# The opening of a four-layer decoder: one list of steps for all engines, two more pieces of weights ahead of the second tokens, two subtractions on GpSimd

## The chip, the cores and the metric

The kernel runs on one core of a Trainium2 chip. What counts is the device time of one execution in microseconds. Five engines run their own instruction streams in order: TensorE (matrix products and transposes), VectorE, ScalarE, GpSimd, and SyncE, which here only issues transfers from HBM. They wait for each other through semaphores.

## The reference

The whole trunk is four layers over 256 tokens of 1024 values. A layer is a token mixer (attention, short convolution, gated linear attention, attention again) and a squared-ReLU MLP, each between two RMS norms:

```python
def reference(x, norm_gains, sb_w_qkv, ...):
    h = x
    for i in range(DEPTH):
        kind, j = i % N_MIXERS, i // N_MIXERS
        xn = rms_norm(h, norm_gains[i, 0])
        ...
        h = h + rms_norm(m, norm_gains[i, 1])
        f = squared_relu_mlp(rms_norm(h, norm_gains[i, 2]), ffn_w_up[i], ffn_w_down[i])
        h = h + rms_norm(f, norm_gains[i, 3])
    return h
```

The change lies in the opening: the first norm (`rms_norm(h, norm_gains[0, 0])`) and the first of layer 0's projections, `xn @ w_qkv` for the values, columns 2048 to 3071 of `sb_w_qkv[0]`.

## The kernel before, in words

Everything is in float32. To run products at the fast rate, each operand is split into two parts of lower precision, a rounded upper part (`hi`) and the rest (`lo = raw - hi`), and a product of two matrices becomes three: hi with hi, hi with lo, lo with hi. Weights stream from HBM in pieces of 128 x 1024 (half a megabyte). Each piece lands in one of five `raw` buffers (`next_piece`, line 204, transfer on SyncE's queue at line 219), ScalarE casts it to `hi` (line 232), VectorE subtracts to `lo` (line 242), both in two halves of 512 columns, and TensorE takes the parts from rings of nine buffers. A raw buffer comes free when the subtractions of its piece are done, and only then its next transfer starts.

The 256 tokens are two groups of 128 (`h[0]` and `h[1]`, "first" and "second" tokens below). In the opening (`opening`, line 1008) each group is loaded; its sum of squares is taken half by ScalarE (`sumsq`, line 294) and half by VectorE (line 1034); one over the root follows (`rstd_on_act`: a small addition on GpSimd, line 287, then Ln and Exp on ScalarE, lines 288 and 289; for the second group `rstd_of`: line 277 on VectorE and a power on GpSimd, line 278); VectorE scales the group (line 1040), TensorE turns it in two halves of four 128 x 128 transposes (line 323) into PSUM, ScalarE rounds it with the gains to `xth` (line 1050) and VectorE forms the rest `xtl` (line 1057). Then the value projection runs: 8 pieces of weights, 2 groups, three kinds of products (hh: `xth` with `hi`; hl: `xth` with `lo`; lh: `xtl` with `hi`), and two halves of 512 columns, 96 products in all, into two accumulators of PSUM. Where nothing real is ready, TensorE runs fillers (`keep_busy`), products of a tile of ones with a tile of zeros. GpSimd fills four tiles with zeros at the start (line 581) and is almost idle after.

The order of the opening on VectorE, ScalarE, TensorE and SyncE is the order in which the code is written, inside `tc.manual_schedule`; the rest of the kernel is ordered by the scheduler. After the opening come the queries' and keys' projections, which start with piece 8 of the weights.

The lines of the opening that set the order around the change:

```python
            pieces.append(next_piece())
            nc.sync.dma_start(out=h[1], in_=xv[1])
            upper(0)
            pieces[0][1](0)
            first, second = halves_squared(1)
            pieces[0][1](1)
            r = rstd_of(first, 1, second)
            rounded(0, 0)
            rest_of(0, 0)
            in_order("hh00 hl00 lh00")
            normed(1, 0, r)
            normed(1, 1, r)
```

## Time and profile before

| what | us |
|---|---|
| median of three runs | 1175.03 (1174.85 to 1176.07) |
| the profiled execution | 1174.96 |
| span of its instructions | 1173.2 |
| TensorE busy | 1164.6 (99%) |
| VectorE busy | 813.5 (69%) |
| ScalarE busy | 678.1 (58%) |
| GpSimd busy | 43.8 (4%) |
| first product of the opening starts | 8.95 |
| first product of the queries starts | 32.04 |

The span is the time from the first to the last instruction of the program. The rows further down are of five kinds: the page's busy shares, the timelines of single engines (consecutive instructions of one line are merged into a row with their count), groups of instructions with their mean length, the range of lengths of one line's instructions, and the time from a transfer's issue to its landing.

### The profile page before, as it was taken

How to read it: one execution, taken by the hardware profiler on the slowest of the kernel's cores; microseconds unless marked ns; L12 is line 12 of the kernel's file. 1: busy time of each engine (PE TensorE's matmuls, PEld its weight loads, DVE VectorE, ACT ScalarE, POOL GpSimd, SP SyncE). 2: the span in 40 equal slices, each digit the busy share in tenths (PEclk: the TensorE clock that was granted, in tenths of full speed). 3: DMA queues.
4: the chain of work that ended last, by engine and by line, in shares of the span. 5: the costliest groups of instructions: out<-in, count | busy, mean ns of one | idle time of the engine just before them, and what ended most of it. 6: DMA issues, size and time to landing. Idle time of an engine off the chain costs nothing.

```text
span 1173.2 us, 17278 instructions
## 1 busy us (share of the span) xinstructions
PE 1164.6 (99%) x6424; PEld 1004.0 (86%) x6424; DVE 813.5 (69%) x1299; ACT 678.1 (58%) x1255; POOL 43.8 (4%) x84
## 2 busy tenths in 40 slices
PE   9999999999999999999999999999999999999997
PEld 7998888888888888888889888888888998888886
DVE  7875876664877786665777778657658776855652
ACT  6886655543655564554584756545546875644541
POOL 1000100000100100000101010000000001000000
PEclk9999999999999999999999999999999999999999
DMA  8743676666576476666473536666647444666640
GB/s 270 240 145 106 187 243 185 195 194 181 168 237 204 146 235 196 185 195 220 143 228 107 178 122 217 194 191 193 208 147 230 135 144 135 222 192 191 190 149 36
DMA packets 126185, 213.65 MB, mean 182 GB/s; under 512 B 10955, under 2 KB 89043, under 8 KB 126101
## 3 DMA queue, kind: packets, MB, share of 16 engines
q1 hardware_dynamic: 125620, 211.95, 58.1%
q8 instruction: 50, 0.82, 0.3%
q10 hardware_dynamic: 448, 0.59, 0.1%
q14 instruction: 35, 0.28, 0.1%
q0 software_dynamic: 32, 0.00, 0.0%
HBM read 211.48 MB, written 1.05 MB: 181 GB/s over the span
## 4 chain that ended last, share of the span: by engine, by line
PE 97%; ACT 1%; DMA 0%; DVE 0%; issue 0%; SPq 0%; DVEq 0%; ACTq 0%
PE acc L119 71%; PE wk L119 24%; PE wk L323 2%; ACT hi L234 0%; DMA h<-in_x_dram 0%; ACT hi L232 0%; ACT s L944 0%; ACT s L294 0%; DVE s L829 0%; DVE lo L242 0%; ACT s L268 0%; ACT s L819 0%; ACT s L817 0%; SPq L219 0%; SPq L130 0%
## 5 line engine op out<-in xcount | busy, mean ns | idle before, releaser
L242 DVE TENSOR_TENSOR lo<-raw,hi 128x512 fp32r<-128x512 f32 x752 | 491.8, 686 | 207.2 <-ACT hi L232 204.4
L232 ACT CAST hi<-raw 128x512 fp32r<-128x512 f32 x752 | 438.4, 620 | 313.2 <-PE acc L119 172.1
L119 PE MATMUL acc<-hi,s 128*128 128x512 f32 x1216 | 339.5, 391 | 0.1
L119 PEld LDWEIGHTS acc<-hi,s 128*128 128x128 f32 x1216 | 225.1, 188 | 46.1 <-ACT s L268 0.8
L119 PE MATMUL wk<-xt,hi 128*128 128x256 f32 (+1 forms) x1120 | 248.7, 309 | 0.0
L119 PE MATMUL wk<-xt,lo 128*128 128x256 f32 x704 | 196.9, 280 | 0.0
L119 PEld LDWEIGHTS wk<-xt,hi 128*128 128x128 f32 x1120 | 181.8, 188 | 13.4 <-ACT s L805 0.3
L119 PE MATMUL acc<-lo,s 128*128 128x512 f32 x608 | 190.4, 390 | 0.0
L119 PE MATMUL acc<-xt,hi 128*128 128x512 f32 x512 | 179.6, 393 | 0.0
L119 PE MATMUL acc<-hi,xt 128*128 128x512 f32 x576 | 159.9, 394 | 0.1
L119 PE MATMUL acc<-xt,lo 128*128 128x256 f32 x512 | 143.2, 280 | 0.0
L119 PEld LDWEIGHTS acc<-lo,s 128*128 128x128 f32 x608 | 114.0, 188 | 23.8
L119 PEld LDWEIGHTS wk<-xt,lo 128*128 128x128 f32 x704 | 132.3, 188 | 0.0
L119 PEld LDWEIGHTS acc<-hi,xt 128*128 128x128 f32 x576 | 106.2, 188 | 23.1 <-ACT xt L268 1.4
L119 PEld LDWEIGHTS acc<-xt,hi 128*128 128x128 f32 x512 | 96.1, 188 | 21.0
L119 PEld LDWEIGHTS acc<-xt,lo 128*128 128x128 f32 x512 | 96.2, 188 | 0.9
L119 PE MATMUL acc<-lo,xt 128*128 128x512 f32 x288 | 89.2, 391 | 0.0
L119 PEld LDWEIGHTS acc<-lo,xt 128*128 128x128 f32 x288 | 54.0, 188 | 11.4
L309 DVE TENSOR_TENSOR s<-acc,s 128x1024 f32<-128x1024 f32 (+1 forms) x16 | 19.0, 1190 | 57.5 <-ACT s L294 57.3
L275 POOL TENSOR_SCALAR sm<-sm 128x1 f32<-128x1 f32 x29 | 13.7, 471 | 1038.5 <-ACT s L294 1038.5
L294 ACT ACTIVATE s<-acc 128x1024 f32<-128x1024 f32 (+1 forms) x16 | 16.0, 999 | 55.4 <-PE acc L119 55.4
L119 PE MATMUL acc<-s,s 128*128 128x256 f32 (+4 forms) x298 | 39.3, 317 | 0.4 <-DVE s L829 0.2
(136 smaller groups left out, 882.2 us busy)
## 6 DMA issues: line engine op xcount, KB each, us to landing
raw<-in_ffn_w_up_dram SPq DMA_DIRECT2D x128, 512.0 KB, 4.0
raw<-in_ffn_w_down_dram SPq DMA_DIRECT2D x128, 512.0 KB, 3.7
raw<-in_sb_w_qkv_dram SPq DMA_DIRECT2D x47, 512.0 KB, 4.8
raw<-in_conv_w_in_dram SPq DMA_DIRECT2D x24, 512.0 KB, 4.8
raw<-in_gla_w_in_dram SPq DMA_DIRECT2D x24, 512.0 KB, 3.9
raw<-in_sb_w_o_dram SPq DMA_DIRECT2D x16, 512.0 KB, 3.9
s<-in_norm_gains_dram SPq DMA_DIRECT2D x15, 512.0 KB, 5.5
raw<-in_conv_w_out_dram SPq DMA_DIRECT2D x8, 512.0 KB, 4.3
```

The lines of the kernel that those rows point to most:

```text
L119: nc.tensor.matmul(out=o, lhsT=l, rhs=r, start=start, stop=stop, skip_group_check=True)
L232: nc.scalar.copy(out=hi[:, cs], in_=raw[:, cs])
L242: nc.vector.tensor_tensor(out=lo[:, cs], in0=raw[:, cs], in1=hi[:, cs].bitcast(F32), op=ALU.subtract)
L275: nc.gpsimd.tensor_scalar(out=v, in0=ss, scalar1=EPS, scalar2=None, op0=ALU.add)
L294: nc.scalar.activation(out=scratch()[:, 0:src.shape[1]], in_=src, func=AF.Square, scale=1.0 / 32.0, accum_out=ss)
L309: nc.vector.tensor_tensor(out=ag[:, cs], in0=a, in1=g[:, cs], op=ALU.mult)
L323: nc.tensor.transpose(out=dst[:, j * P:(j + 1) * P], in_=src[:, j * P:(j + 1) * P], identity=ident)
```

## The change

The opening is now driven by one string, `ORDER`. Each word is a step: `ld` a piece's transfer, `h00` the transfer of the second tokens, `q` half a sum of squares, `r` the root, `n` a scaling, `f` four transposes, `g` and `gt` the gains' transpose and copy, `z` fillers, `u` and `d` one rounding and one rest of 128 columns, `hi` and `lo` one half of a cast and of a subtraction, `po` a subtraction on GpSimd, and `hh`, `hl`, `lh` one product (piece, group of tokens, half). GpSimd is now among the engines whose order is the list's. Two lines of the table stand for it:

```diff
+ORDER = " ".join((
+    "ld00 ld10 ld20 h00 ld30 ld40 q0a q0b z06 g00 r00 n00 gt00 hi00 z02 f00 lo00 hi01 u00 n01 u01 lo01 ld50 hh000 u02",
+    "hh001 u03 hl000 hi10 d00 hl001 f01 d01 hi11 d02 lh100 d03 hi20 lo10 lh101 po11 ld60 hh100 hi21 hh101 lh000 lh001",
...
-    for cs in (slice(0, 512), slice(512, D)):
+
+    cuts = [(slice(0, n), slice(n, D)) for n in (640, 512)]
+    for cs in cuts[0]:
         nc.sync.dma_start(out=h[0][:, cs], in_=xv[0][:, cs])
     cfl = T(cp, [P, C_A], F32, "cf")
-    nc.scalar.dma_start(out=cfl[:, 0:P], in_=const_f[:, 0:P])
+    nc.sync.dma_start(out=cfl[:, 0:P], in_=const_f[:, 0:P])
...
-        def lower(j):
+        def lower(j, eng=nc.vector):
...
-            nc.vector.tensor_tensor(out=lo[:, cs], in0=raw[:, cs], in1=hi[:, cs].bitcast(F32), op=ALU.subtract)
-
-        return upper, lower
+            eng.tensor_tensor(out=lo[:, cs], in0=raw[:, cs], in1=hi[:, cs].bitcast(F32), op=ALU.subtract)
+
+        return upper, lower, partial(lower, eng=nc.gpsimd)
...
+        def product(which, t, k, n):
+
+
+            seen[t, n] = seen.get((t, n), 0) + 1
+            mm(banks(accs[t])[n], xs(t)[which == "lh"][k], wide((l, "v"), k)[n][which == "hl"],
+               seen[t, n] == 1, seen[t, n] == 3 * KT)
+
+        def step(word):
...
+            elif what == "r":
+                factor[t] = rstd_on_act(sums[t, "b"], 1, sums[t, "a"])
...
+            elif what in ("u", "d"):
+                (rounded if what == "u" else rest_of)(t, int(at[1]))
+            elif what in ("hi", "lo", "po"):
+                pieces[t][("hi", "lo", "po").index(what)](int(at[1]))
...
         with tc.manual_schedule(engines={mybir.EngineType.DVE, mybir.EngineType.Activation, mybir.EngineType.PE,
-                                         mybir.EngineType.SP}):
+                                         mybir.EngineType.SP, mybir.EngineType.Pool}):
             nc.vector.memset(still.bitcast(F32), 0.0)
-            keep_busy(STILL[0])
...
+            for word in ORDER.split():
+                step(word)
             rest_of_constants()
             ahead[0] = RAMP[0]
```

So the transfers go out as: first tokens (640 and 384 columns), the identity's constants, pieces 0, 1 and 2, second tokens, pieces 3 and 4; before, they were first tokens (512 and 512), piece 0, second tokens, pieces 1, 2 and on, with the constants on ScalarE's queue. The fillers are 6 + 2 instead of 5 + 4 + 4. The root of the second tokens now takes the way of the first (addition on GpSimd, Ln and Exp on ScalarE). The second halves of pieces 1 and 2 are subtracted on GpSimd. The number of products, transposes, casts and roundings is the same. After the opening, the instructions of each engine stand in the order of before but for a half cast or two.

On GpSimd, from the last of the four fills on, this stands before (`sm` are columns of 128 single values; L287 is the addition for the first tokens, L278 the power for the second, L275 already belongs to the end of the layer's mixer):

```order
L581 MEMSET s_103 128x1024
L287 ISA
L287 TENSOR_SCALAR sm_134<-sm_128 128x1 [waits Activation_49]
L278 TENSOR_TENSOR sm_169<-sm_170,mhalf_91 128x1 [waits DVE_49]
L275 TENSOR_SCALAR sm_1379<-sm_1374 128x1 [waits Activation_49]
```

and this now (L305 is the addition, for the first tokens and for the second; L260 the subtraction; raw_121 and raw_125 are pieces 1 and 2):

```order
L599 MEMSET s_103 128x1024
L305 ISA
L305 TENSOR_SCALAR sm_152<-sm_138 128x1 [waits Activation_49]
L260 TENSOR_TENSOR lo_124<-raw_121,hi_123 128x512 [waits DMAHW6_49,Activation_49]
L260 TENSOR_TENSOR lo_128<-raw_125,hi_127 128x512 [waits DMAHW7_49,Activation_49]
L305 TENSOR_SCALAR sm_223<-sm_208 128x1 [waits Activation_49]
```

The two subtractions stand between the additions of the first and of the second tokens.

On VectorE, from the gains' copy to the second tokens' scaling, this stands before (h_80 and h_81 are the first and second tokens, sm_110 the gains, raw_154 piece 0, wk_139 the first turned half of the first tokens):

```order
L1093 COPY sm_110<-wk_121 128x8 [waits PE_49]
L1034 SCALAR_TENSOR_TENSOR s_106,sm_131<-h_80 128x512 [waits DMAHW1_49]
L1040 TENSOR_SCALAR s_111<-h_80,sm_133 128x512 [waits DMAHW0_49,Activation_49]
L1040 TENSOR_SCALAR s_111<-h_80,sm_133 128x512
L242 TENSOR_TENSOR lo_158<-raw_154,hi_157 128x512 [waits DMAHW3_49,Activation_49]
L1034 SCALAR_TENSOR_TENSOR s_106,sm_166<-h_81 128x512 [waits DMAHW6_49,DVE_49]
L242 TENSOR_TENSOR lo_158<-raw_154,hi_157 128x512 [waits DMAHW5_49,Activation_49]
L277 TENSOR_SCALAR sm_170<-sm_163,sm_166 128x1 [waits DVE_49,Activation_49]
L1057 SCALAR_TENSOR_TENSOR xt_94<-wk_139,sm_110,xt_94 128x128 [waits Activation_49]
L1057 SCALAR_TENSOR_TENSOR xt_94<-wk_139,sm_110,xt_94 128x128 x3
L1040 TENSOR_SCALAR s_112<-h_81,sm_169 128x512 [waits Pool_49]
```

and this now (raw_116, raw_121 and raw_125 are pieces 0, 1 and 2, wk_161 the first turned half):

```order
L1089 SCALAR_TENSOR_TENSOR s_106,sm_141<-h_80 128x384 [waits DMAHW1_49]
L1095 TENSOR_SCALAR s_111<-h_80,sm_151 128x512 [waits DMAHW0_49,Activation_49]
L1106 COPY sm_110<-wk_149 128x8 [waits PE_49]
L260 TENSOR_TENSOR lo_120<-raw_116,hi_119 128x512 [waits DMAHW4_49,Activation_49]
L1095 TENSOR_SCALAR s_111<-h_80,sm_151 128x512
L260 TENSOR_TENSOR lo_120<-raw_116,hi_119 128x512 [waits DMAHW5_49,Activation_49]
L1057 SCALAR_TENSOR_TENSOR xt_94<-wk_161,sm_110,xt_94 128x128 [waits DVE_49,Activation_49]
L1057 SCALAR_TENSOR_TENSOR xt_94<-wk_161,sm_110,xt_94 128x128 x3
L260 TENSOR_TENSOR lo_124<-raw_121,hi_123 128x512 [waits DMAHW6_49,Activation_49]
L1089 SCALAR_TENSOR_TENSOR s_106,sm_211<-h_81 128x512 [waits DMAHW0_49]
L260 TENSOR_TENSOR lo_128<-raw_125,hi_127 128x512 [waits DMAHW7_49,Activation_49]
L1095 TENSOR_SCALAR s_112<-h_81,sm_222 128x512 [waits Activation_49]
```

The gains' copy moved behind the first scaling, and the second tokens' squares (s_106 from h_81) moved behind the rests of the first tokens and the first subtraction of piece 1.

On TensorE, ahead of the second tokens' first transposes, this stands before (acc_107 is the accumulator of the first tokens, hi_157 and hi_191 belong to pieces 0 and 1, wk_199 is the second tokens' first turned half; two products stand in front of these rows):

```order
L119 MATMUL acc_107<-lo_158,xt_94 128x512 [waits DVE_49] x2
L119 MATMUL acc_107<-hi_157,xt_94 128x512 [waits DVE_49]
L119 MATMUL acc_107<-hi_157,xt_94 128x512
L119 MATMUL acc_107<-hi_191,xt_94 128x512 [waits Activation_49] x2
L119 MATMUL acc_107<-hi_191,xt_94 128x512 [waits DVE_49]
L119 MATMUL acc_107<-hi_191,xt_94 128x512
L323 MATMUL wk_199<-cf_84,s_112 128x128 [waits DVE_49]
```

and this now (hi_119, hi_123 and hi_127 belong to pieces 0, 1 and 2, wk_234 is the second tokens' first turned half; four products and the four transposes of the first tokens' second half stand in front of these rows):

```order
L135 MATMUL acc_107<-hi_123,xt_94 128x512 [waits DVE_49,Activation_49]
L135 MATMUL acc_107<-hi_123,xt_94 128x512 [waits Activation_49]
L135 MATMUL acc_107<-hi_123,xt_94 128x512 x2
L135 MATMUL acc_107<-hi_119,xt_94 128x512 x2
L135 MATMUL acc_107<-hi_127,xt_94 128x512 [waits DVE_49,Activation_49]
L135 MATMUL acc_107<-hi_127,xt_94 128x512 [waits Activation_49]
L135 MATMUL acc_107<-lo_124,xt_94 128x512 [waits DVE_49]
L135 MATMUL acc_107<-lo_124,xt_94 128x512 [waits Pool_49]
L135 MATMUL acc_107<-hi_127,xt_94 128x512 x2
L135 MATMUL acc_107<-lo_128,xt_94 128x512 [waits DVE_49]
L135 MATMUL acc_107<-lo_128,xt_94 128x512 [waits Pool_49]
L341 MATMUL wk_234<-cf_84,s_112 128x128 [waits DVE_49]
```

All products of pieces 0, 1 and 2 that need only the first four slices of the first tokens now stand ahead of the second tokens' transposes, 18 instead of 10, and two of them wait for GpSimd.

## Rows read from the trace of the kernel before

**Rows 1.** The page's first part: busy us, share of the span, count.

```profile
PE 1164.6 (99%) x6424; PEld 1004.0 (86%) x6424; DVE 813.5 (69%) x1299; ACT 678.1 (58%) x1255; POOL 43.8 (4%) x84
```

**Rows 2.** Timeline of TensorE, 0 to 45: start, length, instruction, count, [idle].

```profile
1.84 2.50 PE L119 MATMUL acc<-s,onesr 128*128 128x512 f32 x5 [1.84 <-DVE s L1089]
...
4.48 2.08 PE L119 MATMUL acc<-s,onesr 128*128 128x512 f32 x4
6.56 1.41 PE L323 MATMUL wk<-cf,s 128*128 128x128 f32 x8
...
8.95 0.73 PE L119 MATMUL acc<-hi,xt 128*128 128x512 f32 x2
...
28.87 0.62 PE L119 MATMUL acc<-lo,xt 128*128 128x512 f32 x2
29.32 1.07 PE L119 MATMUL acc<-hi,xt 128*128 128x512 f32 x4
...
32.04 0.40 PE L119 MATMUL wk<-xt,hi 128*128 128x256 f32 x2
```

**Rows 3.** Timeline of ScalarE in the opening.

```profile
5.46 0.29 ACT L288 ACTIVATE sm<-sm,sm 128x1 f32<-128x1 f32 x1 [1.07 <-DVE s L1034]
...
6.67 0.62 ACT L232 CAST hi<-raw 128x512 fp32r<-128x512 f32 x1 [0.18 <-DMA raw<-in_sb_w_qkv_dram]
7.92 0.63 ACT L294 ACTIVATE s<-h 128x512 f32<-128x512 f32 x1 [0.63 <-DMA h<-in_x_dram]
...
8.55 1.12 ACT L1050 ACTIVATE xt<-wk,sm 128x128 fp32r<-128x128 f32 x4
9.55 2.19 ACT L232 CAST hi<-raw 128x512 fp32r<-128x512 f32 x4
```

**Rows 4.** Timeline of VectorE in the opening.

```profile
1.02 0.73 DVE L140 CAST onesr<-mones 128x128 fp32r<-128x128 f32 x1
...
4.58 0.17 DVE L1093 COPY sm<-wk 128x8 f32<-128x8 f32 x1 [2.79 <-PE wk L1092]
4.67 0.68 DVE L1034 SCALAR_TENSOR_TENSOR s<-h 128x512 f32<-128x512 f32 x1
...
6.02 0.88 DVE L1040 TENSOR_SCALAR s<-h,sm 128x512 f32<-128x512 f32 x2 [0.66 <-ACT sm L289]
...
25.35 0.22 DVE L1006 CAST cr<-cf 128x128 fp32r<-128x128 f32 x1
```

**Rows 5.** Landing of the first tokens' second half: issue, and time from it.

```profile
L130 SPq DMA_DIRECT2D h<-in_x_dram x1: 420/420/420, 1.2 to 1.2; - x1
...
DMA to landing us min/median/max: 3.2/3.2/3.2
```

**Rows 6.** Landing of piece 2, the same view.

```profile
L219 SPq DMA_DIRECT2D raw<-in_sb_w_qkv_dram x1: 328/328/328, 3.7 to 3.7; - x1
...
DMA to landing us min/median/max: 6.7/6.7/6.7
```

**Rows 7.** GpSimd's groups: busy us, mean ns, idle; the last alone at 614.

```profile
L581 POOL MEMSET s<- 128x1024 f32 x4 | 3.7, 970 | 0.3 <-POOLq L1173 0.3
...
L287 POOL TENSOR_SCALAR sm<-sm 128x1 f32<-128x1 f32 x2 | 0.4, 221 | 4.2 <-ACT s L294 4.1
...
L858 POOL TENSOR_SCALAR s<-s 128x64 f32<-128x64 f32 x1 | 0.5, 458 | 0.3 <-ACT s L854 0.3
```

**Rows 8.** Timeline of GpSimd, 881 to 883.

```profile
881.44 1.15 POOL L275 TENSOR_SCALAR sm<-sm 128x1 f32<-128x1 f32 x1 [3.44 <-ACT s L294]
```

**Rows 9.** Timeline of VectorE in the same stretch.

```profile
880.69 1.21 DVE L332 TENSOR_TENSOR s<-h,s 128x1024 f32<-128x1024 f32 x1
881.83 0.68 DVE L242 TENSOR_TENSOR lo<-raw,hi 128x512 fp32r<-128x512 f32 x1
```

**Rows 10.** Timeline of GpSimd in the opening: the four fills.

```profile
0.72 3.69 POOL L581 MEMSET s<- 128x1024 f32 x4 [0.29 <-POOLq L1173]
```

**Rows 11.** Line 899 on VectorE: shortest, median, longest in ns, first, last start.

```profile
L899 DVE TENSOR_TENSOR s<-s,s x28: 412/418/458, 620.8 to 642.5; 128x256 f32<-128x256 f32 x28
```

More of the change, by code (lines that the diff above doesn't have):

```diff
@@ L1061, in opening @@
-        pieces = []
-        def upper(*js):
-            for j in js:
-                while len(pieces) <= j:
-                    pieces.append(next_piece())
-                for n in range(PS):
-                    pieces[j][0](n)
-        def lower(*js):
-            for j in js:
-                for n in range(PS):
-                    pieces[j][1](n)
-        def products(which, t, *js):
-            for j in js:
-                stat = xs(t)[which == "lh"][j]
-                for n, w in enumerate(wide((l, "v"), j)):
-                    mm(banks(accs[t])[n], stat, w[which == "hl"], which == "hh" and j == 0, which == "hl" and j == KT - 1)
@@ new lines, in opening @@
+        pieces = []
+        sums = {}
+        factor = {}
+        seen = {}
+        def product(which, t, k, n):
[3 more added lines that the diff above has]
+        def step(word):
+            what, at = word[:-2], (int(word[-2]), word[-1])
+            t = at[0]
+            if what == "ld":
+                pieces.append(next_piece())
+            elif what == "h":
+                nc.sync.dma_start(out=h[1], in_=xv[1])
+            elif what == "q":
+                cs = cuts[t][at[1] == "b"]
+                if at[1] == "a":
+                    sums[t, "a"] = sumsq(h[t][:, cs])
+                else:
+                    sums[t, "b"] = small()
+                    nc.vector.scalar_tensor_tensor(out=jk[:, cs], in0=h[t][:, cs], scalar=1.0 / D, in1=h[t][:, cs],
+                                                   op0=ALU.mult, op1=ALU.mult, accum_out=sums[t, "b"])
+            elif what == "r":
+                factor[t] = rstd_on_act(sums[t, "b"], 1, sums[t, "a"])
+            elif what == "n":
+                cs = sides[int(at[1])]
+                nc.vector.tensor_scalar(out=xns[t][:, cs], in0=h[t][:, cs], scalar1=factor[t], scalar2=None,
+                                        op0=ALU.mult)
+            elif what == "f":
+                half = int(at[1])
+                halves[t, half] = wk_tile()
+                transposes(xns[t][:, half * 512:], halves[t, half], 4)
+            elif what == "g":
+                gw = wk_tile()
+                nc.tensor.transpose(out=gw[:, 0:KT], in_=g8, identity=ident[0:KT, 0:KT])
+                halves["g"] = gw
+            elif what == "gt":
+                nc.vector.tensor_copy(out=gt, in_=halves["g"][:, 0:KT])
+            elif what == "z":
+                keep_busy(int(at[1]))
+            elif what in ("u", "d"):
+                (rounded if what == "u" else rest_of)(t, int(at[1]))
+            elif what in ("hi", "lo", "po"):
+                pieces[t][("hi", "lo", "po").index(what)](int(at[1]))
+            else:
+                product(what[:2], t, int(what[2]), int(at[1]))
@@ L1094, in opening @@
-            keep_busy(STILL[1])
-            first, second = halves_squared(0)
-            r = rstd_on_act(second, 1, first)
-            for half in range(2):
-                normed(0, half, r)
-                flipped(0, half)
-            keep_busy(STILL[2])
-            pieces.append(next_piece())
-            nc.sync.dma_start(out=h[1], in_=xv[1])
-            upper(0)
-            pieces[0][1](0)
-            first, second = halves_squared(1)
-            pieces[0][1](1)
-            r = rstd_of(first, 1, second)
```

77 lines of the change are left out of this document (13 added, 64 removed), and 7 rows, old and new, of the table ORDER.

## The prediction

> **What bounds the kernel now.** I read the page's busy shares first: TensorE is busy 1164.6 of 1173.2 us [rows 1]. With everything after the opening bound by TensorE, and the same products left in it, the change can only move the moment at which the opening's last product is done. So the next view is TensorE's timeline of the opening [rows 2]: fillers until 8.95, where the first product of weights and tokens starts, then products and transposes almost without a hole until 32.04, where the queries' products begin. That 32.04 is the number to move. The opening holds 96 products (2 groups of 128 tokens, 8 pieces of weights, three kinds, two halves), and two lo products and the next row start 0.455 us apart (28.87 to 29.32), so one costs 0.2275 and all 21.8 of the 23.1 us between 8.95 and 32.04. There are two ways to gain: start the first product earlier, and lose nothing in between.
>
> Why is 8.95 the start? ScalarE's timeline [rows 3] shows it: the rounding of the first tokens (L1050) starts at 8.55, behind the square of the second tokens (L294 at 7.92), which had itself waited for their landing. VectorE's timeline [rows 4] shows the second cause, farther up: its sum of squares (L1034) starts at 4.67, behind the copy of the gains at 4.58, though the second half of the first tokens had landed at 1.2 + 3.2 = 4.4 [rows 5].
>
> **The change part by part.** I replay each engine's new order with the durations of the rows.
>
> *Statistics of the first tokens.* The gains' copy now stands behind the first scaling, and VectorE sums 384 columns instead of 512: 0.68 x 384/512 = 0.5 us from 4.3, so the Ln that ran at 5.46 runs at about 4.9, and the first scaling at 5.4 instead of 6.02. Four transposes follow at about 5.95, while scaling and handover took 6.56 - 6.02 = 0.54 before. The constants of the identity now come third on SyncE's queue instead of on ScalarE's; the bytes ahead of piece 0 are the same in sum, so I leave its second half at 6.65, where its cast began at 6.67. The cast takes 0.52 of ScalarE's time (four in 2.19, the last 0.62 long), so rounding starts at 7.2 and its first result comes 0.37 later. **First product: 7.6**, 1.35 us earlier.
>
> *Landing of the second tokens.* Pieces 1 and 2 now go ahead of them. They landed at 7.9 as the third transfer of half a megabyte; piece 2, two places on, landed at 3.7 + 6.7 = 10.4 [rows 6]. The second tokens take that place: 10.4. Their square on ScalarE is done at about 11.15.
>
> *Pieces 1 and 2.* ScalarE casts piece 1 right behind four roundings (0.25 apart, four in 1.12): 7.2 + 1.0 = 8.2 and 8.7, done at 9.35; piece 2 is done at 10.4. TensorE has 18 products and four transposes for the first tokens to do before it needs the second: 7.6 + 18 x 0.2275 + 4 x 0.11 + two handovers of 0.15 = 12.45. That is when the transposes of the second tokens' first half are wanted.
>
> *The two subtractions on GpSimd.* They leave VectorE 2 x 0.6 us less to do, but VectorE isn't what is late here. On GpSimd they stand in front of the small addition (0.22) that the second tokens' Ln waits for. So a new chain sets the second tokens: the two subtractions, then addition 0.25, Ln and Exp 0.53 (5.46 to 6.02 with its handover), scaling and handover 0.54, in all 1.34 from the end of the second subtraction to the transposes. What is queued behind it: on ScalarE the casts of piece 3 behind the Ln, on VectorE the scaling, on TensorE all 78 products left.
>
> What one subtraction costs on GpSimd no row shows. From below: a fill of 1024 columns takes 0.97 and reads nothing, so 512 columns take 0.5. From above: a one-operand instruction on 64 columns took 0.458, one on one column 0.22, so 0.0037 a column, 0.22 + 511 x 0.0037 = 2.1 for 512 [rows 7]. I take **1.17**: the fixed 0.22 and two operands of 512 columns at that fill's rate, 0.95 for 1024 columns. It is nearest to that row, since the 64 columns are too few to tell the slope from the start. The Trainium skill (GPSIMD Engine Reference, section 3.1) gives 4497 ns for 2048 columns of such an instruction; a quarter would be an estimate of 1.12 and a sum 0.1 lower, and no run here shows it.
>
> *The two engines hold each other up.* GpSimd's L275 at 881.44 took 1.15 us for one column that elsewhere takes 0.22: VectorE ran two instructions with both operands in SBUF, from 880.69 and from 881.83 to 882.51, and GpSimd ended 0.08 after the second [rows 8, 9]. The other way round, VectorE's cast of 128x128 took 0.73 at 1.02, while GpSimd filled tiles from 0.72 on, and 0.22 at 25.35, with GpSimd idle [rows 4, 10]. So I let them alternate, one whole instruction each. First subtraction: wanted at 9.4, held by VectorE's subtraction of piece 1 until 9.65, done at 10.8. VectorE's squares of the second tokens wanted 10.4, go at 10.8 and hold 0.6. Second subtraction: 11.4 to 12.6. Transposes of the second tokens: 12.6 + 1.34 = **13.9**, 1.5 later than TensorE wants them. The products of piece 2's low part, whose halves come from VectorE and from GpSimd, wait in the same place and add nothing.
>
> The Trainium skill (SBUF — State Buffer, section Who interferes with whom) says that whoever starts first has the shared port for its whole instruction, against GpSimd instructions that read. One row speaks for less: VectorE's L899 took 458 ns at most against 418 in the median of 28, among which GpSimd's 64-column instructions read [rows 11]. A hold of 0.04 for 64 columns is some 0.6 for a subtraction; the squares then start at 10.4, the transposes at 13.5, and the sum would be +0.2. By the rule it is the sum below.
>
> *Sum.* After the transposes' start there are 78 products and eight transposes: 78 x 0.2275 + 8 x 0.11 + 0.1 = 18.74. So the opening ends at 13.92 + 18.74 = 32.66 against 32.04: **+0.6 us**. In general it ends at 30.32 + 2p, for a subtraction of p; break-even is p = 0.86. What comes next in line, the order of the rest, is the same as before, and pieces 8 onward are wanted by TensorE only from 32 us on, some 7 us behind their casts. The profiled execution of before took 1174.96 us (span 1173.2, 1.8 around it), 0.07 under the median of 1175.03, so the forecast is 1174.96 + 0.6 = **1175.6**.
>
> **The rivals.** A measurement of this kernel can tell about 0.2%, 2.35 us, from no change.
>
> *Nothing held, or a quick subtraction.* If the engines don't hold each other up at p = 1.17, the chain is 9.4 + 2.34 + 1.34 = 13.1, and the opening ends at 31.8: -0.2, 1174.8. At p = 0.5 the next late one is VectorE's last subtraction in the list, of piece 5's second half, behind eight others and eight roundings: -0.3. With nothing late at all, 7.6 + 96 x 0.2275 + 12 x 0.11 + 0.3 = 31.1, or -0.95: even that is within 0.2%. For it speaks the L899 row, against it the other two pairs.
>
> *Slower: GpSimd at the upper price.* With p = 2.06 and the engines held, 30.32 + 4.12 = 34.4, +2.4: 1177.4, just past 0.2%; it decides from p = 2.04. For it speaks the 64-column row, against it the fill's rate.
>
> *TensorE stays at its lower clock.* The page's clock line reads full from the start, but the four fillers from 4.48 take 2.08 us and so start 0.43 apart, the 1.2 GHz level; products at 8.95 start at twice that pace, the 2.4 GHz level, and TensorE had not paused since 1.84. The change has eight fillers instead of thirteen, and TensorE would stand idle for about 0.2, 0.3 and 0.8 us before the first product. If the clock rises by 10.7, the wait at 13.9 hides it all. If it rises only at 14, the 18 products cost 0.43 each and the second tokens' work is pushed to about 15: +1.7, 1176.7.
>
> *The change doesn't do what it says.* If piece 0 lands later than 6.65, the first product is later too, and the chain on GpSimd with it, one for one; 0.3 us of it gives 1175.9, inside the forecast.
>
> **How the numbers follow.** The forecast, held engines and p from 0.9 to 1.6, has 0.64; nothing held or quick, 0.18; the upper price, 0.09; the late clock, 0.09. The likeliest is 1175.6. For the range I leave out the end below -0.7, which needs both a quick subtraction and nothing late, and take the upper price in: 1174.3 to 1177.4; the three runs of before alone lie 1.2 apart. Faster by over 0.2% is beyond even the floor of -0.95: 0.03, for what I overlooked. Slower by over 0.2% needs p over 2.04, or a late clock with a slow GpSimd: 0.11. The same: 0.86.
>
> **What would show it.** Right: first product near 7.6; GpSimd's two subtractions near 1.2 each, ending about 12.6; a hole of 1 to 1.7 us on TensorE before the transposes of the second tokens, ended by VectorE's subtraction or scaling; the queries' first product at about 32.7. Wrong: no hole there (nothing held, p below 0.9), products 0.43 apart after 7.6 (the clock), a hole elsewhere, above all in the last products of piece 5, or second tokens that land far from 10.4.

## The result and the profile after

The changed kernel is slower by a little: 1177.07 us in the median of 16 executions (1175.91 to 1180.31) against 1175.53 in 16 of the kernel before (1174.84 to 1176.47). The ratio is 1.0016, with an interval from 1.0009 to 1.0022, so some 1.5 us where +0.6 was forecast. The one trace that came with the result is of the slowest of the sixteen executions (1180.31, span 1178.5), so the changed kernel was profiled a second time (run *again* below: 1177.57 in the median of 11, its traced execution 1178.05 with a span of 1176.3). Both traces are read here; both are of executions slower than the median.

The page's first part, after [rows 1]:

```profile
PE 1166.0 (99%) x6419; PEld 1005.3 (85%) x6419; DVE 813.5 (69%) x1296; ACT 679.5 (58%) x1257; POOL 47.1 (4%) x86
```

TensorE in the opening and behind it, after, first trace [rows 2] (start, length, instruction, count, idle time ahead and what ended it):

```profile
6.03 0.66 PE L341 MATMUL wk<-cf,s 128*128 128x128 f32 x4
8.41 0.72 PE L135 MATMUL acc<-hi,xt 128*128 128x512 f32 x2 [1.72 <-ACT xt L1052]
...
10.44 3.02 PE L135 MATMUL acc<-hi,xt 128*128 128x512 f32 x8
...
15.49 0.66 PE L341 MATMUL wk<-cf,s 128*128 128x128 f32 x4 [0.42 <-DVE s L1095]
...
34.18 0.40 PE L135 MATMUL wk<-xt,hi 128*128 128x256 f32 x2
...
48.96 3.60 PE L135 MATMUL acc<-s,s 128*128 128x256 f32 x18 [1.95 <-ACT s L286]
```

The same in the second trace (*again*):

```profile
7.95 0.73 PE L135 MATMUL acc<-hi,xt 128*128 128x512 f32 x2 [1.28 <-ACT xt L1052]
...
9.46 2.22 PE L135 MATMUL acc<-hi,xt 128*128 128x512 f32 x8
...
13.87 0.73 PE L135 MATMUL acc<-lo,xt 128*128 128x512 f32 x2 [1.26 <-DVE lo L260]
15.02 0.66 PE L341 MATMUL wk<-cf,s 128*128 128x128 f32 x4 [0.42 <-DVE s L1095]
...
35.31 0.40 PE L135 MATMUL wk<-xt,hi 128*128 128x256 f32 x2
...
47.99 2.59 PE L135 MATMUL acc<-s,s 128*128 128x256 f32 x18
```

Two rows of the kernel before that answer to them: the second tokens' transposes, and the products of queries with keys (the last 12 of 18), which need the keys' rounding:

```profile
11.61 0.60 PE L323 MATMUL wk<-cf,s 128*128 128x128 f32 x4
...
45.89 1.70 PE L119 MATMUL acc<-s,s 128*128 128x256 f32 x12 [0.18 <-DVE s L269]
```

GpSimd's pair in the second trace:

```profile
9.84 3.42 POOL L260 TENSOR_TENSOR lo<-raw,hi 128x512 fp32r<-128x512 f32 x2 [4.97 <-ACT hi L250]
```

| us | before | after | again |
|---|---|---|---|
| first product | 8.95 | 8.41 | 7.95 |
| second tokens' transposes | 11.61 | 15.49 | 15.02 |
| queries' first product | 32.04 | 34.18 | 35.31 |
| wait before the products at 46 to 49 | 0.18 | 1.95 | none shown |
| span | 1173.2 | 1178.5 | 1176.3 |

So the first product came 0.5 to 1.0 earlier, and everything behind it lost more than that. The granted clock (windows of TensorE: stretch, length, busy, count, clock, transfers' share, GB/s; first trace, then the second):

```profile
9.10:12.40 3.30, 3.30 (x12) 0.50 1.01 410
...
50.10:53.40 3.30, 3.30 (x17) 0.50 0.95 332
```

```profile
15.80:19.20 3.40, 3.40 (x10) 0.50 0.58 189
```

In the first trace the clock fell to half, 1.2 GHz, behind the idle 1.72 us and again behind the idle 1.95; in the second it stayed at the upper level behind the idle 1.28 and fell behind the waits of 1.26 and 0.42. Eight products then took 3.02 us at 10.44 where *again* shows 2.22 at 9.46, and 18 products 3.60 where *again* shows 2.59. For the second trace the loss up to the queries, 3.27, is the whole of the span's 3.1. For the first it is 2.14, and the second wait (1.95 - 0.18) and the slow products behind it (3.60 - 2.59, and a few more) make up the rest of 5.3. The first trace's fall in the opening cost nothing there: TensorE still waited 0.42 for the scaling at 15.49, and from there to the queries it took 18.69. The second trace's fall came behind the transposes: 20.29 from there to the queries, 1.6 more.

ScalarE, VectorE and GpSimd, first trace [rows 3, 4, 10]:

```profile
4.93 0.29 ACT L306 ACTIVATE sm<-sm,sm 128x1 f32<-128x1 f32 x1 [0.34 <-POOL sm L305]
...
7.47 0.62 ACT L250 CAST hi<-raw 128x512 fp32r<-128x512 f32 x1 [0.80 <-DMA raw<-in_sb_w_qkv_dram]
8.00 1.14 ACT L1052 ACTIVATE xt<-wk,sm 128x128 fp32r<-128x128 f32 x4
9.31 2.39 ACT L250 CAST hi<-raw 128x512 fp32r<-128x512 f32 x4 [0.18 <-DMA raw<-in_sb_w_qkv_dram]
11.82 0.63 ACT L312 ACTIVATE s<-h 128x512 f32<-128x512 f32 x1
...
14.38 0.30 ACT L306 ACTIVATE sm<-sm,sm 128x1 f32<-128x1 f32 x1 [1.84 <-POOL sm L305]
...
46.32 1.14 ACT L250 CAST hi<-raw 128x512 fp32r<-128x512 f32 x2 [1.84 <-DVE lo L260]
```

```profile
10.21 0.68 DVE L260 TENSOR_TENSOR lo<-raw,hi 128x512 fp32r<-128x512 f32 x1
11.82 0.76 DVE L1089 SCALAR_TENSOR_TENSOR s<-h 128x512 f32<-128x512 f32 x1 [0.93 <-DMA h<-in_x_dram]
...
12.52 1.77 DVE L260 TENSOR_TENSOR lo<-raw,hi 128x512 fp32r<-128x512 f32 x1
14.95 0.49 DVE L1095 TENSOR_SCALAR s<-h,sm 128x512 f32<-128x512 f32 x1 [0.67 <-ACT sm L307]
```

```profile
10.53 3.20 POOL L260 TENSOR_TENSOR lo<-raw,hi 128x512 fp32r<-128x512 f32 x2 [5.64 <-ACT hi L250]
13.81 0.53 POOL L305 TENSOR_SCALAR sm<-sm 128x1 f32<-128x1 f32 x1
```

The second tokens' squares start at 11.82, their Ln waits 1.84 us for GpSimd's small addition, and that stands behind the two subtractions, which end at 13.73. VectorE's subtraction of piece 2 took 1.77 instead of 0.68.

### The profile page after: what moved, and what is told of

Its sections match the earlier page's. It is cut to its first block, busy times and chain, and to the rows that moved or that the text cites. A ratio compares the mean times of both kernels' runs of the same rounds, so it can differ in the third digit from the quotient of the medians.

```text
span 1178.5 us, 17278 instructions
## 1 busy us (share of the span) xinstructions
PE 1166.0 (99%) x6419; PEld 1005.3 (85%) x6419; DVE 813.5 (69%) x1296; ACT 679.5 (58%) x1257; POOL 47.1 (4%) x86
## 4 chain that ended last, share of the span: by engine, by line
PE 95%; ACT 1%; DVE 1%; issue 1%; DMA 1%; POOL 0%; SPq 0%; DVEq 0%; ACTq 0%
PE acc L135 70%; PE wk L135 23%; PE wk L341 2%; DVE lo L260 1%; DMA raw<-in_sb_w_qkv_dram 1%; ACT hi L252 0%; ACT hi L250 0%; POOL lo L260 0%; ACT s L962 0%; DVE s L847 0%; DVE s L611 0%; ACT s L286 0%; ACT s L837 0%; ACT s L835 0%; SPq L237 0%
## 5 line engine op out<-in xcount | busy, mean ns | idle before, releaser
L260 DVE TENSOR_TENSOR lo<-raw,hi 128x512 fp32r<-128x512 f32 x750 | 492.1, 687 | 213.3 <-ACT hi L250 210.5
```

The costliest lines, as they stand in the source:

```text
L260: eng.tensor_tensor(out=lo[:, cs], in0=raw[:, cs], in1=hi[:, cs].bitcast(F32), op=ALU.subtract)
```

## The experiments

Each kernel was timed beside the kernel before, in four groups of runs; the medians of the kernel before were 1175.73 (*again* to *ordered*), 1175.57 (*vec_ord* to *vec_ord_xt_queue*), 1175.38 (*xt_only* to *best_cold*) and 1175.81 (the last three). The ratio in brackets is against it. A difference between runs of two groups carries this shift of up to 0.4. A time is the median of 11 executions. Edits of the list are shown by the words around them.

**again**: the changed kernel, unchanged. 

> The changed kernel as it is, profiled once more: its one trace is of the slowest of its executions (1180.31 us beside a median of 1177.07), so it may show more than the usual loss. Theory L (the loss is lasting): the time is 1177 again, TensorE idles 1.5 to 2 us before its first product at about 8.4, the granted clock falls to 0.5 for some 3 us behind that, the queries' first product starts at 33.5 to 34.2 (32.04 before), and TensorE idles again for 1 to 2 us before the keys' rounding at 47 to 49. Theory O (that trace is an odd one out): one or both of the idle stretches is under 0.5 us, and the clock doesn't fall again.

Measured 1177.57 (ratio 1.0017, 1.0008 to 1.0026). The loss is lasting. The two traces differ in where the clock fell and in the second wait; the first wait (1.28) and the late second tokens (15.02) are in both.

**fill**

```diff
-hi00 z02 f00 lo00
+hi00 z02 f00 z06 lo00
```

> Six more 128x512 fillers on TensorE, between the first tokens' first four transposes and the first product, where it idled 1.72 us: six at 0.2275 are 1.37 us, all inside the hole. Theory C (the lower clock behind the hole is the largest part of the opening's loss: 8 products took 3.02 us at 10.44 where 1.82 is their time at the upper clock, and the products and transposes ahead of them lost about as much again in part): the clock stays at 1.0 through 9 to 13 us, the queries' first product comes 1 to 1.7 us earlier than in the changed kernel, and the time is about 1175.5 to 1176. Theory S (supply: second tokens' scaling and the weights set the end of the opening, whatever the clock): TensorE is early and waits longer at the second tokens' transposes at 15.5, and the time stays at 1177.

Measured 1178.08 (1.0022, 1.0013 to 1.0031). TensorE, start to first product:

```profile
6.37 1.05 PE L341 MATMUL wk<-cf,s 128*128 128x128 f32 x4
7.07 2.62 PE L135 MATMUL acc<-s,onesr 128*128 128x512 f32 x6
9.53 0.63 PE L135 MATMUL acc<-hi,xt 128*128 128x512 f32 x2
```

The products behind 9.53 ran at the upper pace, as theory C wanted, but in this execution the fillers themselves ran at the lower one (0.43 each) and held the first product up until 9.53. Even so the transposes stand at 14.71 and the opening ends at 33.36, earlier than in both traces above; then TensorE waits 1.20 at 47.40. The median didn't fall, and why is not seen here, since the trace is of the fastest of the eleven executions (1177.45). Theory C isn't shown by this run. Its GpSimd and VectorE serve below as a price: GpSimd wasn't held in either subtraction (1.29 and 1.30), and the squares, started less than 0.1 behind the second one, took 1.78.

```profile
10.38 2.55 POOL L260 TENSOR_TENSOR lo<-raw,hi 128x512 fp32r<-128x512 f32 x2 [5.43 <-ACT hi L250]
```

```profile
11.70 1.78 DVE L1089 SCALAR_TENSOR_TENSOR s<-h 128x512 f32<-128x512 f32 x1 [1.20 <-DMA h<-in_x_dram]
```

**vector**

```diff
-lh101 po11 ld60
+lh101 lo11 ld60
...
-q1b po21 lh201
+q1b lo21 lh201
```

> The two subtractions of the changed kernel that stand on GpSimd go to VectorE, at the same places in the order; nothing else. In the trace of the changed kernel the pair took 3.20 us on GpSimd and one VectorE subtraction beside it 1.77 us, and the second tokens' scaling started at 14.95. Theory G (the pair on GpSimd sets the second tokens): the scaling starts 0.8 to 1.3 us earlier, the idle 0.42 us before the second tokens' transposes goes, the time falls by 0.4 to 1 us to about 1176.3. Theory C: those transposes are late mostly since the clock is low from 9 to 12.5 us, and the time falls by 0.4 at most, to 1176.7 to 1177.1. The holes downstream (47 to 49 us) stay under both.

Measured 1176.43 (1.0005, 0.9997 to 1.0014), 1.1 below *again*: theory G. The second tokens' transposes start at 14.73 with no wait ahead of them, and the opening ends at 33.34. The wait at 47 shrank too, to 0.53, which neither theory had.

**ordered**

```diff
-lo50 lh210 hi70 lh211 f11 hi71 hl010 hl011 u14 lo71
+lo40 lh210 hi60 lh211 f11 hi61 hl010 hl011 u14 lo41
...
-lo41 lh111 hi60 lh310 lh311 lo40 hi61
+lo50 lh111 hi70 lh310 lh311 lo51 hi71
...
-lo70 lh410 lh411 lo61
+lo61 lh410 lh411 lo70
...
-lo51
+lo71
```

> The changed kernel with the castings and subtractions of the last four pieces of the opening in the order in which the pieces are loaded (4, 5, 6, 7; they stand as 5, 7, 4, 6, 7, 6, 5 in the list). Nothing else moves. A load needs one of five buffers, which comes free with the last subtraction of the piece five before it: the load of piece 9 was issued at 23.47 us (18.53 before), piece 10 at 25.70 (23.26 before). Theory D (the late buffers set the weights behind and with them the second hole, 1.95 us before 48.96 and the lower clock behind it): the load of piece 9 is issued at about 19 to 20, ScalarE's waits of 2.23, 1.69 and 2.14 us for weights at 26 to 33 us shrink, the hole before 49 us is under 0.5 us, and the time is 1.5 to 3 us below the changed kernel, 1174 to 1175.5. Theory E (the second hole comes from the end of the opening being later or from something else): the hole stays over 1.5 us and the time is at 1177.

Measured 1176.86 (1.0010, 1.0002 to 1.0019), 0.7 below *again*. Issue of piece 9 on SyncE's queue, kernel before, after, and *ordered* (lengths in ns, first and last start in us):

```profile
L219 SPq DMA_DIRECT2D raw<-in_sb_w_qkv_dram x1: 379/379/379, 18.5 to 18.5; - x1
```

```profile
L237 SPq DMA_DIRECT2D raw<-in_sb_w_qkv_dram x1: 379/379/379, 23.5 to 23.5; - x1
```

```profile
L237 SPq DMA_DIRECT2D raw<-in_sb_w_qkv_dram x1: 374/374/374, 21.3 to 21.3; - x1
```

The list frees piece 4's buffer 5 us later than the kernel before did. In order, half of that comes back, and TensorE shows no wait ahead of its 18 products at 47.19. *again* shows none either, so this one trace doesn't decide between the theories, and the time is nearer to theory E's 1177 than to theory D's; the opening itself still ends 2.5 us late (34.51). All the traces together speak for theory D: with the change's order of the last subtractions a wait of 0.5 to 1.95 us stands ahead of the 18 products in four of six (not in *again* and *best_late*), with the loads' order in none of ten. In this execution TensorE ran at the lower level ahead of its idle 1.71 (four transposes in 1.06 instead of 0.66) and at the upper level behind it, where the first trace shows the reverse:

```profile
8.75 0.74 PE L135 MATMUL acc<-hi,xt 128*128 128x512 f32 x2 [1.71 <-ACT xt L1052]
...
10.26 2.17 PE L135 MATMUL acc<-hi,xt 128*128 128x512 f32 x8
```

**vec_ord**: the last two edits together. 

> Two edits together: the two subtractions of GpSimd go to VectorE, and the castings and subtractions of the last four pieces of the opening stand in the order of their loads. Against the changed kernel (1177.6 in the last call) the first alone measured 1176.4, the second alone 1176.9. Theory of two places (the pair on GpSimd makes the opening end later, the late buffers make the hole before the keys' rounding; what one adds comes on top of the other): the gains add, 1.1 + 0.7, and the time is about 1175.7, with the second tokens' transposes at 14.2 to 14.8, no wait over 0.3 us at 46 to 49 us. Rival, one place (the order of subtractions only makes good what the pair had delayed): 1176.4 again, since the pair is gone already.

Measured 1175.94 (1.0004, 0.9995 to 1.0012): nearer to the sum, 1175.7, than to the rival; single executions lie between 1174.81 and 1177.84, so the two are not told apart for certain. In its trace (1177.20) the transposes stand at 16.08 instead of 14.2 to 14.8, though the scaling was done at 14.2: the products ahead of them ran at half pace up to 14.7. The row of the granted clock reads 1.00 there; the products' pace shows it:

```profile
11.31 3.54 PE L135 MATMUL acc<-hi,xt 128*128 128x512 f32 x8
```

**vec_ord_xt**

```diff
-f00 lo00 hi01 u00 n01
+f00 lo00 u00 hi01 n01
...
-hh001 u03 hl000 hi10
+hl000 u03 hh001 hi10
```

> As vec_ord, and on ScalarE the rounding of the first tokens' first block stands ahead of the casting of piece 0's second half, and TensorE's product of the lower half stands ahead of that of the second half. In the traces the first product waited 1.3 to 1.8 us for a rounding that stood behind a casting that waited for the second half to land (7.0 to 7.8 us). Now the first product should start at about 7.1 and the idle time be three pieces of some 0.4 us. Theory C (the idle stretch before the first product lowers the clock, and that costs up to 1.7 us): the clock is 1.0 through 8 to 13 us in the trace, the opening ends 1 to 1.5 us earlier than in vec_ord (below 32.5), and the time falls by 0.6 to 1.5 us against it. Theory S (weights' landing sets the opening): TensorE then idles about as long before piece 1's or the second tokens' products, and the time falls by 0.3 at most.

Measured 1175.05 (0.9994, 0.9986 to 1.0003), 0.9 below *vec_ord*; the spread of *vec_ord* reaches over both. The first product comes at 7.81 with 0.46 of idle time ahead instead of 1.62, and the opening ends at 32.47 instead of 34.72. By their pace the products reach the upper level at about 9.6 here, so most of the difference between the two traces is the clock; that the shorter wait brought it is theory C, and not shown by two executions.

**vec_ord_tok**

```diff
-ld00 ld10 ld20 h00 ld30
+ld00 h00 ld10 ld20 ld30
```

> As vec_ord, and the load of the second tokens stands ahead of pieces 1 and 2 again, behind piece 0, as it did in the kernel before: they should land at about 9.3 to 9.8 instead of 11.1 to 12.2, and pieces 1 and 2 some 1.25 us later each (10.2 to 10.9 and 11.5 to 12.1). Theory T (the second tokens' way is the longest): their transposes come 1 to 2 us earlier, the time falls by 0.4 to 1 us against vec_ord. Theory P (it is the pieces that TensorE wants first, and the order of its products is made for them): TensorE idles about 1 us before the products of piece 1, and the time is 0 to 1 us above vec_ord.

Measured 1176.98 (1.0008, 0.9999 to 1.0017), 1.0 above *vec_ord*, as theory P has it, but with both spreads this wide not clear of noise. No gain shows. Theory T isn't tested fully: the second tokens landed at 8.9 (issued at 3.06, 5.8 before landing), yet their squares began only at 12.00, since the edit moves the transfer and not the steps, and VectorE still does pieces 0 and 1 first. So the two pieces ahead of the second tokens show as no part of the loss with the list's order on the engines.

**vec_ord_xt_queue**, called the mended opening from here on:

```diff
-    nc.sync.dma_start(out=cfl[:, 0:P], in_=const_f[:, 0:P])
+    nc.scalar.dma_start(out=cfl[:, 0:P], in_=const_f[:, 0:P])
```

> As vec_ord_xt, and the transfer of the identity is issued on ScalarE's queue, as it was before the change, instead of on SyncE's between the first tokens and piece 0 (one issue there is 0.42 us). Theory Q (that issue delays every transfer behind it): piece 0's second half lands at 6.6 to 7.0 instead of 7.0 to 7.8, pieces 1 and 2 and the second tokens 0.4 to 0.5 us earlier, and the time falls by 0.3 to 0.5 us against vec_ord_xt. Theory N (the transfers share the same 16 engines whichever queue issues them): landings and the time stay within 0.2 us.

Measured 1174.81 (0.9994, 0.9985 to 1.0003), 0.24 below *vec_ord_xt*, which its spread doesn't tell from nothing. In its trace piece 0's second half landed at 6.6 instead of 6.9, but the first tokens' squares on VectorE began at 4.71 instead of 4.18, behind their landing. Its TensorE, and GpSimd's addition for the second tokens:

```profile
7.61 0.50 PE L135 MATMUL acc<-hi,xt 128*128 128x512 f32 x1 [0.46 <-ACT xt L1052]
...
9.63 2.17 PE L135 MATMUL acc<-hi,xt 128*128 128x512 f32 x8
...
13.64 0.60 PE L341 MATMUL wk<-cf,s 128*128 128x128 f32 x4
...
32.26 0.40 PE L135 MATMUL wk<-xt,hi 128*128 128x256 f32 x2
```

```profile
11.62 0.26 POOL L305 TENSOR_SCALAR sm<-sm 128x1 f32<-128x1 f32 x1 [6.27 <-ACT s L312]
```

**xt_only**: the edit of *vec_ord_xt* alone, on the changed kernel. 

> The changed kernel with one edit alone: the first tokens' first rounding ahead of the casting of piece 0's second half on ScalarE, and the product of the lower half ahead of that of the second half on TensorE. The pair on GpSimd and the order of the last subtractions stay as the change has them. Theory of three places (the wait before the first product, the pair on GpSimd and the late buffers each cost their own part): the time falls by about as much as this edit gave beside the two others, 0.9 us, from 1177.3 to 1176.4, with the first product at 7.5 to 7.9. Rival (the pair alone sets when the second tokens come, so what is gained ahead of it is lost waiting for it): TensorE idles 2 us or more in front of the products and transposes that wait for the pair, from 11.5 to 15 us, and the time is 1177 to 1177.5.

Measured 1177.33 (1.0017, 1.0008 to 1.0026): the rival. TensorE then waits 1.25 and 0.42 us for the pair and the scaling, and the transposes stand at 15.61. The wait ahead of the first product shrank to 0.46, but the product itself came at 8.02, hardly earlier than the 8.41 and 7.95 above. What the run shows is that a shorter wait there is worth nothing while GpSimd's chain sets the second tokens.

**best_pair**: the mended opening with `po11` and `po21` back on GpSimd. 

> The fastest kernel so far (vec_ord_xt_queue, 1174.8) with the pair of subtractions on GpSimd again, and nothing else: what the pair costs where all else is mended. In the traces of the changed kernel and of fill, again and ordered the pair took 2.55 to 3.50 us, and the addition in front of the second tokens' scaling stood behind it on GpSimd. Theory G: the scaling comes 1.2 to 2 us later (at 14 to 14.8 where it was about 12.5), TensorE idles 1 to 1.7 us before 15, the time is 1175.8 to 1176.5. Rival (the lead of the opening hides the pair): 1174.8 to 1175.2.

Measured 1176.88 (1.0014, 1.0005 to 1.0023), 2.07 above the mended opening (2.3 with each taken against the kernel before beside it): theory G, above its range. One of the eleven executions took 6659.3 us and stays unexplained; the others lie between 1176.51 and 1178.20. VectorE and GpSimd:

```profile
11.15 1.55 DVE L1089 SCALAR_TENSOR_TENSOR s<-h 128x512 f32<-128x512 f32 x1
...
12.63 1.76 DVE L260 TENSOR_TENSOR lo<-raw,hi 128x512 fp32r<-128x512 f32 x1
15.06 0.49 DVE L1095 TENSOR_SCALAR s<-h,sm 128x512 f32<-128x512 f32 x1 [0.67 <-ACT sm L307]
```

```profile
10.36 3.49 POOL L260 TENSOR_TENSOR lo<-raw,hi 128x512 fp32r<-128x512 f32 x2 [5.06 <-ACT hi L250]
13.93 0.53 POOL L305 TENSOR_SCALAR sm<-sm 128x1 f32<-128x1 f32 x1
```

The scaling starts at 15.06 where the mended opening has 12.94, the transposes at 15.60 where it has 13.64, and the opening ends at 34.28 where it has 32.26. TensorE ran at half pace up to 13.8 here, but still waited 0.28 for the scaling, so the pair sets these 2.0.

**best_late**: the mended opening with the change's order of the last subtractions. 

> The fastest kernel so far with the last subtractions and castings in the order of the change (5, 7, 4, 6, 7, 6, 5) again, and nothing else. Theory D (late buffers make the hole before the keys' rounding, whatever the opening does): the load of piece 9 is issued at 20.5 to 22 instead of 18.8, and since TensorE is earlier here than in the changed kernel the hole before the keys' rounding at 45 to 48 us is 1 to 2.5 us; the time is 1175.6 to 1177. Rival (the hole came from executions in which the opening had gone wrong): under 0.3 us of hole, and 1174.8 to 1175.1.

Measured 1175.14 (0.9999, 0.9990 to 1.0007), 0.3 above the mended opening (0.5 with each taken against the kernel before beside it); piece 9 is issued at 21.4 instead of 18.8, yet no wait is shown ahead of the 18 products at 44.86. Nearer to the rival: the order alone costs little here. In *vector*, with the same order and the subtractions on VectorE too, piece 9 was issued at 22.7 and 0.53 of wait was left.

**best_cold**: the mended opening without its eight fillers.

```diff
-q0b z06 g00
+q0b g00
...
-hi00 z02 f00
+hi00 f00
```

> The fastest kernel so far without the eight fillers on TensorE at 1.8 to 6 us, so that TensorE has no work before the gains' transpose at 4.7 and next to none before the first tokens' transposes at 6.5: the granted clock should be at 0.5 until some time behind the first product (it was 0.5 until 14.1 to 14.5 in two traces whose first product came at 8.6 to 8.7). There 8 products took 3.44 to 3.54 us where 2.17 is their time at the upper level. Theory C (the lower clock costs what it lengthens): the opening ends 1 to 2 us later than 32.26 and the time is 1175.8 to 1176.8. Theory S (the opening waits for weights and second tokens anyway, so the slower products only fill its waits): at most 0.4 us later, 1174.8 to 1175.2.

Measured 1175.76 (1.0003, 0.9994 to 1.0012), 0.95 above the mended opening (1.15 with each taken against the kernel before beside it): at theory C's lower end, 1175.8, and well over S. TensorE:

```profile
9.82 1.05 PE L341 MATMUL wk<-cf,s 128*128 128x128 f32 x4
10.53 3.11 PE L135 MATMUL acc<-hi,xt 128*128 128x512 f32 x8
```

The first product starts at 7.95, the eight products take 3.11 instead of 2.17, the opening ends at 33.50 instead of 32.26. This is the price of the lower clock where nothing else hides it, about 1 us; the mended opening itself is not at the upper level in every execution (*best_again* below).

**best_sum_first**: as *best_pair*, with the second tokens' addition ahead of the second subtraction on GpSimd.

```diff
-q1b po21 lh201
+q1b lh201
...
-ld70 r10 hh200
+ld70 r10 po21 hh200
```

> As best_pair (1176.88; 1174.81 without the pair), but on GpSimd the addition in front of the second tokens' scaling stands ahead of the second subtraction of the pair, not behind it. In best_pair's trace the second tokens' squares were both summed by 12.7 us, the addition started at 13.93, behind the pair, and took 0.53 us (0.27 without the pair), so that the scaling started at 15.06. Theory Q (what costs is the queue: the addition stands behind the pair on its engine): the addition is done at 12.5, the scaling starts at 13.4 to 14.2, the time falls by 0.8 to 1.6 us to 1175.3 to 1176.1. Theory H (what costs is that VectorE and GpSimd hold each other, so that the pair's time is taken from VectorE wherever it stands): the second subtraction now holds the scaling itself or the lower half that TensorE wants next, and the time falls by 0.4 us at most.

Measured 1175.71 (1.0001, 0.9992 to 1.0009), 1.17 below *best_pair* (1.6 with each taken against the kernel before beside it): theory Q. VectorE and GpSimd:

```profile
10.60 1.77 DVE L1089 SCALAR_TENSOR_TENSOR s<-h 128x512 f32<-128x512 f32 x1
...
13.04 1.39 DVE L1095 TENSOR_SCALAR s<-h,sm 128x512 f32<-128x512 f32 x1
```

```profile
11.91 0.54 POOL L305 TENSOR_SCALAR sm<-sm 128x1 f32<-128x1 f32 x1
12.53 1.62 POOL L260 TENSOR_TENSOR lo<-raw,hi 128x512 fp32r<-128x512 f32 x1
```

The scaling now starts at 13.04, held itself by the second subtraction (1.39 instead of 0.49), and is done at 14.43 where it was done at 15.55.

**best_one**: as *best_pair*, with `po21` back on VectorE and `po11` on GpSimd. 

> As best_pair, but only the first subtraction of the pair (piece 1's second half) stands on GpSimd; the second goes to VectorE. Theory H says that one half of the pair costs about half: VectorE and GpSimd then have the same instructions to share one after the other, but one at 1.15 to 1.3 us instead of 0.6; the time is 1175.5 to 1176. Theory Q: the addition stands behind one subtraction that ends at 12.1, before the second tokens' squares are summed at 11.6 to 12.7, so that nothing waits for it and the time is 1174.8 to 1175.2.

Measured 1175.74 (1.0001, 0.9992 to 1.0010): theory H's number. Even one subtraction on GpSimd, with VectorE's squares held beside it, costs some 0.8 against the mended opening:

```profile
10.92 1.79 DVE L1089 SCALAR_TENSOR_TENSOR s<-h 128x512 f32<-128x512 f32 x1
```

So the pair's 2.1 to 2.3 us is 0.7 to 0.9 for the first, by holding VectorE, and 1.1 to 1.6 for the second; *best_sum_first* gives as much back by the addition's place alone.

**best_again**: the mended opening, unchanged. 

> The kernel vec_ord_xt_queue once more, unchanged: its median was 1174.81, the kernel before's 1175.57 in that call, with an interval of the ratio from 0.9985 to 1.0003. If it is faster than the kernel before, the median is again 0.4 to 0.8 us below it; if that was the draw of one call, they are within 0.3 us.

Measured 1175.03 beside 1175.81 of the kernel before (0.9996, 0.9987 to 1.0005). Both times its median is 0.8 below the kernel before, and each interval just includes no difference. Its 22 executions lie between 1174.61 and 1175.47, the 60 beside them of the kernel before between 1174.55 and 1177.15. That it beats the changed kernel, by over 2 us, is plain; that it beats the kernel before is likely and not shown. In this trace (1175.43) TensorE idled 0.97 and 0.46 us ahead of its first product and ran at 0.50 from 8.3 to 11.7, and the opening ended at 32.84; in the first trace of the same kernel it idled 0.70 and 0.46 there, the clock stayed up, and the opening ended at 32.26.

## Why the prediction was right and wrong

- *What bounds the kernel, and that the end of the opening is the number to move*: right, but not complete. The lead put behind it ("some 7 us behind their casts") failed: it was read off the kernel before, while the list frees piece 4's and 5's buffers up to 5 us later. In the first trace TensorE waited 1.95 us at 47 to 49 for the keys' rounding, which stands on ScalarE behind casts of weights; the traces of both orders (*ordered*) tie this wait to the late buffers, the single steps between were not followed.
- *Statistics of the first tokens*: right. Ln 4.9 forecast, 4.93 found; first transposes 5.95 and 6.03.
- *Piece 0 stays at 6.65*: wrong. Its second half's cast began at 7.47 and 7.01, and the first product at 8.41 and 7.95 instead of 7.6. The step was "the bytes ahead of piece 0 are the same in sum". The rival of a late piece 0 had it. That the constants' issue in front of it on the same queue is the cause was only argued: it landed at 7.5 and 7.0 with them ahead (6.9 in *vec_ord_xt*) and at 6.6 and 6.9 without in the mended opening's two traces, and moving it back measured 0.24, too little to tell.
- *Second tokens at 10.4*: their squares began at 11.82 and 11.13. With piece 1's casts late too (9.31 instead of 8.2), the subtractions ended at 13.73 and 13.26, not 12.6. Why the same bytes land 0.7 us and more later isn't settled.
- *The price of a subtraction and the held engines*: right. In *fill*, where GpSimd wasn't held, two took 2.55 us, 1.29 each against 1.17 taken. And they alternated: VectorE's instruction beside them took up to 1.79 where it takes 0.68. The Trainium skill's rule (SBUF — State Buffer, Who interferes with whom), that the one that issued first has the shared pair for its whole instruction, agrees with all of these rows; the hold of 0.04 in [rows 11] said nothing of instructions this long.
- *1.34 from the pair to the transposes*: 1.76 in both traces. Missed was that the hold works on GpSimd's addition as well, 0.53 instead of 0.22, because VectorE had taken up its delayed subtraction. (The three parts of the 1.34 add up to 1.32 as written, and the upper price of a subtraction is 2.1 in one place and 2.06 in another; neither moves the forecast.)
- *18.74 from the transposes to the end*: right at the upper clock, 34.18 - 15.49 = 18.69; 20.29 in the second trace, where the clock fell in between.
- *TensorE's clock*: a term that the sum put at nothing. The rival was a clock that rises late, at 0.09. What both traces of the changed kernel show is a clock that falls again behind waits that the change itself makes: worth nothing in the opening of the first trace, where the scaling was later anyway, some 1 us at 50, and 1.6 in the second trace; *best_cold* puts some 1 us on it. The rival itself was seen as well, with the change's eight fillers: in *vec_ord* and *vec_ord_tok* the eight products took 3.54 and 3.44 us.
- *The sum*: forecast 32.66, or +0.6; the median rose by 1.5. The step that failed in both traces is 13.92, the start of the second tokens' transposes: they came at 15.49 and 15.02, 1.6 and 1.1 later. Of that 1.15 and 0.68 is the pair's end, at 13.73 and 13.26 instead of 12.58, mostly for the later landings, and 0.42 the way from there. This alone covers the 0.9 that was missing. The fall of the clock (15.02 + 20.29 = 35.31 in *again*) and the wait for late weights (first trace) came on top in these two executions, whose times are above the median. The mechanism forecast as the loss (a chain of two held subtractions in front of the second tokens) is the one that *best_pair* shows, at 2.1 to 2.3; the prediction's terms make it 1.5 (13.92 - 12.45), of which the earlier first product was to leave 0.6. The time lies inside the range, 1.5 above the forecast time, 0.5 of it because the kernel before itself measured 1175.53 here and not 1175.03.

What stays open: how often each of the two patterns of clock and second wait occurs, since a trace shows one execution; why the transfers land later; and the price of the late buffers, 0.7 in the changed kernel and 0.3 to 0.5 in the mended one, both near what can be told.

## What to carry to other kernels

Work that is handed to an idle engine is not paid by its own length, but by what is queued behind it there (here a one-column addition that half the opening waited for) and by the other engine it holds meanwhile: put the short instruction that others wait for ahead of it. When an order is rewritten by hand, keep the step that frees a buffer in the order of the loads that want it, and move a cast that waits for a transfer behind the work that is ready (0.9 us lower in *vec_ord_xt*, within its spread, and nothing in *xt_only*, where another chain was later). Price a new wait of TensorE at its length and, where nothing later hides them, the slower products behind it.

## What the runs showed of the hardware

- The clock of TensorE fell to 0.50 within one kernel behind waits of 1 to 2 us, and not in each execution: the mended opening idled 0.97 and 0.46 us in *best_again* and ran at 0.50 from 8.3 to 11.7, and idled 0.70 and 0.46 in *vec_ord_xt_queue* without a fall. It also rose at different times with the same eight fillers: by the products' pace at 14.7 us in *vec_ord*, and by 6.0 in the first trace of the changed kernel. The times of one program lie further apart where TensorE waits more, the changed kernel's from 1175.9 to 1180.3, the mended opening's from 1174.6 to 1175.5; that the clock makes this spread is not shown.
- GpSimd and VectorE hold each other in short instructions as in long ones: a GpSimd addition of one column took 0.53 instead of 0.26 beside VectorE's subtraction, and VectorE's scaling, which reads one tile and a column of factors, 1.39 instead of 0.49 beside GpSimd's.
